# A macaron decoder trunk on one core: a fifth token-major group in place of two plain pairs, both down ranges accumulated together, and the first product between the halves of the early pair

## The chip, the cores and the metric

One Trainium2 chip, of which the program uses one core. The metric is device microseconds of one execution. A core has five engines with their own instruction queues: TensorE (PE, matrix products into PSUM banks), VectorE (DVE), ScalarE (ACT), GpSimd (POOL, here mostly an issuer of accumulating transfers) and SyncE (SP, an issuer of transfers).

## The reference

Two layers; each runs a half-step feed-forward network (FFN), a mixing of three kinds of attention, and a second FFN. The change touches the four FFNs (called a0, c0, a1 and c1 here) and one small statistic of `mem`. The sequence has 512 tokens, the model 1024 features, the hidden layer 22 tiles of 128.

```python
def _rmsnorm(t, g):
    t32 = t.astype(jnp.float32)
    t32 = t32 * lax.rsqrt(jnp.mean(t32 * t32, axis=-1, keepdims=True) + RMS_EPS)
    return t32.astype(t.dtype) * g

def _swiglu(t, w_gate, w_up, w_down):
    return (jax.nn.silu(t @ w_gate) * (t @ w_up)) @ w_down

def reference(x, mem, ...):
    mem_n = _rmsnorm(mem, mem_norm_g)
    h = x
    for l in range(DEPTH):
        f = _swiglu(_rmsnorm(h, ffn1_pre_g[l]), ffn1_w_gate[l], ffn1_w_up[l], ffn1_w_down[l])
        h = h + 0.5 * _rmsnorm(f, ffn1_post_g[l])
        ...
        f = _swiglu(_rmsnorm(h, ffn2_pre_g[l]), ffn2_w_gate[l], ffn2_w_up[l], ffn2_w_down[l])
        h = h + 0.5 * _rmsnorm(f, ffn2_post_g[l])
    return h
```

## The kernel before

**Products in three parts.** Every fp32 number is split into a high and a low part (`split`, L185: the high on ACT at L188, the low on DVE at L189), and a product is three matmuls (`mm3`, L212): high by high (L214), high by low (L215), low by high (L216). A weight tile `wh`/`wl` holds 1024 columns per partition, and the rings `wh`, `wl` and `raw` (what the transfer delivers) have four buffers each.

**Gate and up in groups.** Sixteen of the 22 hidden tiles are computed in four groups of four (`TG`, tile f to f+3; names `ta` in FFNs a, `tc` in c). A group is token-major: the tokens are the rows of the result. Gate and up together are one product of a 2 by 2 block matrix, done with seven block products in the manner of Strassen and Winograd instead of eight (`gate_up`; the products n run in `ORDER`, in the first group in `FIRST`). Each is 24 matmuls of 512 columns, 168 in a group. The block differences that products 2, 3, 5 and 6 need of the weights are made by an accumulating transfer on POOL's queue (`kt`, L318) and an addition on DVE (L344); those of the input (`ag`, from `sums`) once in each FFN on DVE and ACT. Results are gathered in tiles `c` (tag f), from PSUM banks of the ring `mm`, and multiplied by silu (L745, L756). `feature_major` then turns the group back with 16 transposes of 128 by 128 (L768), and ACT copies them to the tiles `hr` (L770).

**The rest of gate and up.** The pair of tiles 16 and 17 (`EARLY`, names `pg`, `pu`) runs first, in two halves of 256 tokens (`halved`, 96 matmuls of 256 columns each), while the second half of the tokens is still being normalised and turned (`ut`, `us`). The plain pairs 18 and 20 (`gates`, `ups`: 48 matmuls of 512 columns each) take the tokens in one go: the gates of 18 behind the early pair, its ups within the first down range, pair 20 in two parts within the second.

**Down.** Tiles 0 to 15 go back to the model's width in two ranges of eight tiles, each as seven block products of 24 matmuls (`products`, `product`; weights `wd`, block sums `bt`; factors `first_factor`, `ah`/`al`). Each range accumulates in banks of the ring `z` and adds its results to `fs` (L900 to L902). The last `down` multiplies tiles 16 to 21.

**What sets the order.** Jobs stand in a queue `Q` in the order of the last lines of `ffn` (`some`, `behind`, `add_sums`); a unit of weights is fetched and split some units ahead of its job as buffers come free. A scheduler then places the instructions on each engine, so DVE's and ACT's order follows both the queue and what it takes to be ready first. `chain` in the turns of tokens gives waits (`W_H`, `W_U`) that stand for the time from a residual to a turned tile. `mem_stats` (mean squares of `mem`, with Ln and Exp on ACT) and `mem_norm` run inside a0.

Of the kernel before, what the change touches and what calls it, by code (L numbers as in the profile page):

```python
# [22 lines left out]
def kernel(  # L23
# [79 lines left out]
    BUFS = {"u": 2, "v": 6, "q": 2, "k": 2, "o": 8, "tri": 2, "raw": 4, "rs": 1, "cs": 1, "wh": 4, "wl": 4, "f": 4}  # L103
# [410 lines left out]
    class Sub:  # L514
# [116 lines left out]


    TG = (0, 4, 8, 12)
    EARLY = NC * FC

    HR = ("o", "o", "o", "o", "o", "o", "tri", "tri")
# [3 lines left out]
    def ffn(l, src, wg, wu, wd, dst, name, spare, aside=None):  # L640
# [9 lines left out]
        def silu(f, pg):  # L650
            s = tmp(f"s{name}_{f}")
            nc.scalar.activation(s[:], pg[:], AF.Silu)
            return s

        def hidden(f, pg, pu):
            s = silu(f, pg) if pg is not None else st.pop(("silu", f))
            nc.vector.tensor_tensor(s[:], pu[:], s[:], ALU.mult)
            t = blk("q" if f < EARLY + 2 else "o", f"hid{name}_{f}")
            hid[f] = t[:, 0], t[:, 1]
            split(*hid[f], s[:])  # L660
            if f == NF - 1:
                tc.keep_in_program_order(nc.scalar.preload_act_table_set("natural_log_exp_and_others"))
# [63 lines left out]
        def gate_up(f, n, uns, last_of_top):  # L726
            seeded = ("gb", 1) in st if n == 1 else False
            if n in (0, 1, 2) and not seeded:
                st["gb", SUM[n]] = [pbank("mm", f"pt{name}_{f}_{n}_{e}") for e in range(2)]
# [10 lines left out]
            if n in (0, 2, 3, 6):  # L740
                st["c", i, j] = stile([P, 2, S], "f", f"c{name}_{f}_{i}{j}", F32)
# [12 lines left out]
            if n == 6 or n == last_of_top:  # L754
                u = st["c", i, 1]
                nc.vector.scalar_tensor_tensor(u[:], u[:], -1.0, st["c", i, 0][:], ALU.mult, ALU.mult)  # L756
                st["hid", f, i] = u

        def feature_major(f):

            for i in range(2):
                u = st.pop(("hid", f, i))
                for b in range(2):
                    f2 = f + 2 * b
                    pt = pbank("mm" if f == TG[-1] else "z", f"th{name}_{f2}_{i}")
# [6 lines left out]
                    nc.scalar.copy(pair(f2)[:, :, HALVES[i]], out_)  # L772
# [58 lines left out]
        def gates(f, ug, ahead=False):  # L831
            st[f] = [pbank("mm", f"pg{name}_{f + m}") for m in range(2)]
            for m in range(2):
                yield from gemm(st[f][m][:], ug, m, act)
                if ahead:
                    st["silu", f + m], st[f][m] = silu(f + m, st[f][m]), None

        def ups(f, uu):
            for m in range(2):
                pu = pbank("mm", f"pu{name}_{f + m}")  # L840
                yield from gemm(pu[:], uu, m, act)
                hidden(f + m, st[f][m], pu)

# [929 lines left out]
```

## Time and profile before

| | |
|---|---|
| median of 3 runs | 2379.23 us (2378.88 to 2379.49) |
| the profiled execution | 2378.61 us |
| its span | 2376.9 us, mean TensorE clock 0.998 |
| DMA | 353.92 MB, 149 GB/s on average |
| POOL busy | 189.2 us, 8% of the span |

The span is what the trace covers, and 1.7 us of the execution lie around it. In the profile's rows, "out<-in" names the tiles written and read, with a shape behind them; `x16` means so many instructions in one row. In a row of a timeline the first number is the start in us from the span's start, the second the duration; a bracket tells how long the engine had stood idle and on whom it waited. In a group's row the numbers are total busy us and mean ns of one. In a row of waits stand the total us, the number of times and the longest. A row of windows gives the window, its length, then the busy us (and counts) of PE, PEld (weight loads), DVE, ACT and POOL, the granted TensorE clock, the share of the DMA engines and GB/s. A row of issues gives the count, the size of one and the median us from issue to landing.

### The profile page before, as it was taken

What the parts mean: (1) busy time and instruction counts of PE and PEld (TensorE: products, weight loads), DVE (VectorE), ACT (ScalarE), POOL (GpSimd) and SP (SyncE); (2) the same over time, 40 slices, a digit from 0 to 9 for tenths busy, and PEclk for the clock granted to TensorE, in tenths of its full rate; (3) what the DMA queues carried; (4) which work ended last, traced back from release to release, by engine and by line L of the source; (5) the groups of instructions that cost most, each with busy time, mean ns of one, the idle gap of its engine ahead of it and who ended that gap; (6) DMA issues with size and microseconds to landing.
All of it is one profiled execution on the core that took longest, in us unless ns stands there. A gap on an engine that the chain in (4) does not pass through costs nothing.

```text
span 2376.9 us, 31030 instructions
## 1 busy us (share of the span) xinstructions
PE 2361.9 (99%) x11688; PEld 1996.9 (84%) x11688; DVE 1764.8 (74%) x2436; ACT 1410.3 (59%) x2291; POOL 189.2 (8%) x226
## 2 busy tenths in 40 slices
PE   9999999999999999999999999999999999999998
PEld 8788888888888898888888888888888888888887
DVE  8677877678776677678686788766787766767785
ACT  5656555577665555565655665656675655556654
POOL 1110000001010001100001000000001100011000
PEclk9999999999999999999999999999999999999999
DMA  6776565222223457765657656632232244586563
GB/s 213 205 203 160 152 238 151 71 72 81 76 75 115 151 160 212 190 164 160 210 153 219 178 160 192 206 111 80 63 89 81 71 133 150 161 227 163 159 168 133
DMA packets 234778, 353.92 MB, mean 149 GB/s; under 512 B 10858, under 2 KB 117634, under 8 KB 234116
## 3 DMA queue, kind: packets, MB, share of 16 engines
q1 hardware_dynamic: 208416, 301.57, 39.0%
q0 software_dynamic: 26208, 50.37, 12.4%
q8 instruction: 92, 1.51, 0.3%
q14 instruction: 58, 0.48, 0.1%
q10 hardware_dynamic: 4, 0.00, 0.0%
HBM read 337.22 MB, written 14.68 MB: 148 GB/s over the span
## 4 chain that ended last, share of the span: by engine, by line
PE 96%; DVE 1%; ACT 1%; DMA 1%; issue 0%; DVEq 0%; ACTq 0%
PE ptc L214 4%; PE ptc L216 4%; PE ptc L215 4%; PE pta L214 4%; PE pta L215 4%; PE pta L216 4%; PE pg L214 4%; PE pg L216 4%; PE pg L215 4%; PE pdc L216 3%; PE pda L216 3%; PE pdc L214 3%; PE pda L215 3%; PE pdc L215 3%; PE pda L214 3%; PE pb L214 2%
## 5 line engine op out<-in xcount | busy, mean ns | idle before, releaser
L214 PE MATMUL pg<-us_a,wh_wg 128*128 128x512 f32 x384 | 151.0, 393 | 0.0
L216 PE MATMUL pg<-us_a,wl_wg 128*128 128x512 f32 x384 | 149.7, 390 | 0.0
L215 PE MATMUL pg<-us_a,wh_wg 128*128 128x512 f32 x384 | 149.6, 390 | 0.0
L189 DVE TENSOR_TENSOR wl_tc<-ktc,wh_tc 128x1024 fp32r<-128x1024 f32 x64 | 78.3, 1223 | 54.4 <-ACT wh_tc L188 54.4
L189 DVE TENSOR_TENSOR wl_ta<-kta,wh_ta 128x1024 fp32r<-128x1024 f32 x64 | 78.3, 1223 | 51.4 <-ACT wh_ta L188 51.3
L214 PE MATMUL pta<-wh_ta,aga 128*128 128x512 f32 x256 | 101.3, 396 | 3.5 <-ACT ca L745 3.5
L214 PE MATMUL ptc<-wh_tc,agc 128*128 128x512 f32 x256 | 100.3, 392 | 0.0
L215 PE MATMUL pta<-wl_ta,aga 128*128 128x512 f32 x256 | 100.1, 391 | 0.0
L216 PE MATMUL pta<-wh_ta,aga 128*128 128x512 f32 x256 | 99.8, 391 | 0.0
L215 PE MATMUL ptc<-wl_tc,agc 128*128 128x512 f32 x256 | 99.7, 389 | 0.0
L216 PE MATMUL ptc<-wh_tc,agc 128*128 128x512 f32 x256 | 99.3, 389 | 0.0
L188 ACT CAST wh_tc<-ktc 128x1024 fp32r<-128x1024 f32 x64 | 67.5, 1055 | 53.5 <-PE ptc L216 36.5
L188 ACT CAST wh_ta<-kta 128x1024 fp32r<-128x1024 f32 x64 | 67.4, 1054 | 51.1 <-PE pta L216 35.5
L216 PE MATMUL pdc<-wh_dc,alc 128*128 128x512 f32 x224 | 87.4, 390 | 0.0
L216 PE MATMUL pda<-wh_da,ala 128*128 128x512 f32 x224 | 87.4, 390 | 0.0
L214 PE MATMUL pdc<-wh_dc,ahc 128*128 128x512 f32 x224 | 87.3, 390 | 0.0
L214 PE MATMUL pda<-wh_da,aha 128*128 128x512 f32 x224 | 87.3, 390 | 0.0
L215 PE MATMUL pdc<-wl_dc,ahc 128*128 128x512 f32 x224 | 87.2, 389 | 0.0
L215 PE MATMUL pda<-wl_da,aha 128*128 128x512 f32 x224 | 87.2, 389 | 0.0
L216 PEld LDWEIGHTS pg<-us_a,wl_wg 128*128 128x128 f32 x384 | 72.1, 188 | 15.3
L189 DVE TENSOR_TENSOR wl_tc<-raw_tc,wh_tc 128x1024 fp32r<-128x1024 f32 x48 | 58.6, 1223 | 35.2 <-ACT wh_tc L188 34.8
L215 PEld LDWEIGHTS pg<-us_a,wh_wg 128*128 128x128 f32 x384 | 72.2, 188 | 14.1
(541 smaller groups left out, 7594.4 us busy)
## 6 DMA issues: line engine op xcount, KB each, us to landing
raw_wg<-in_w_gate_dram SPq DMA_DIRECT2D x48, 512.0 KB, 3.6
raw_da<-in_ffn_w_down_dram SPq DMA_DIRECT2D x42, 512.0 KB, 3.8
raw_dc<-in_ffn_w_down_dram SPq DMA_DIRECT2D x42, 512.0 KB, 3.5
raw_ta<-in_ffn_w_gate_dram SPq DMA_DIRECT2D x36, 512.0 KB, 5.3
raw_tc<-in_ffn_w_gate_dram SPq DMA_DIRECT2D x36, 512.0 KB, 4.3
kta<-in_ffn_w_up_dram SPq DMA_DIRECT2D x32, 512.0 KB, 6.3
ktc<-in_ffn_w_up_dram SPq DMA_DIRECT2D x32, 512.0 KB, 6.4
raw_wo<-in_w_out_dram SPq DMA_DIRECT2D x24, 512.0 KB, 3.6
```

Source lines behind the costliest of these rows:

```text
L188: both = [nc.scalar.copy(h_ap, src)]
L189: make = lambda: nc.vector.tensor_tensor(l_ap, src, h_ap.bitcast(F32), ALU.subtract)
L214: nc.tensor.matmul(pt, lh, rh, start=start, stop=False, skip_group_check=free)
L215: nc.tensor.matmul(pt, lh, rl, start=False, stop=False, skip_group_check=free)
L216: nc.tensor.matmul(pt, ll, rh, start=False, stop=stop, skip_group_check=free)
```

## The change

1. `TG` has a fifth group, tiles 16 to 19. The early pair is 20 and 21. `gates`, `ups` and the plain pairs are gone. The fifth group's tiles aren't in a down range: `feature_major` splits them at once into high and low for the last `down`, in two parts, one ahead of the first down product and one behind it.
2. The products of both down ranges are interleaved (`DOWN`: n = 0 of range 0, n = 0 of range 1, n = 2 of range 0, and so on) and accumulate in the same banks, so that results leave the banks once. Both ranges' factors lie in one tile of the ring u.
3. Product 0 of the first group stands between the halves of the early pair; its banks are of the ring z, its result tile of the ring rs. Tiles 2 and 3 of the tokens get 3.0 and 4.0 more of wait where `slack` is 0.
4. The ring rs has two buffers, and holds `mem`'s rows in `mem_stats` and `mem_norm`. The table of Ln and Exp is asked for behind the last group's product 6.

```diff
-    ... "rs": 1, "cs": 1, "wh": 4, "wl": 4, "f": 4}
+    ... "rs": 2, "cs": 1, "wh": 4, "wl": 4, "f": 4}
...
-                yield ("wait", W_U[t] + self.slack)
+                yield ("wait", W_U[t] + self.slack + (W_N[t] if self.slack == 0.0 else 0.0))
...
+    W_N = (0.0, 0.0, 3.0, 4.0)
-    TG = (0, 4, 8, 12)
-    EARLY = NC * FC
-    HR = ("o", "o", "o", "o", "o", "o", "tri", "tri")
+    TG = (0, 4, 8, 12, 16)
+    EARLY = NF - 2
+    HR = 8 * ("o",)
...
-                st["gb", SUM[n]] = [pbank("mm", f"pt{name}_{f}_{n}_{e}") for e in range(2)]
+                st["gb", SUM[n]] = [pbank("z" if n == 0 and f == TG[0] else "mm", f"pt{name}_{f}_{n}_{e}") for e in range(2)]
...
-                st["c", i, j] = stile([P, 2, S], "f", f"c{name}_{f}_{i}{j}", F32)
+                st["c", i, j] = stile([P, 2, S], "rs" if n == 0 and f == TG[0] else "f", f"c{name}_{f}_{i}{j}", F32)
...
+            if n == 6 and f == TG[-1]:
+                tc.keep_in_program_order(nc.scalar.preload_act_table_set("natural_log_exp_and_others"))
-        def feature_major(f):
-            for i in range(2):
+        def feature_major(f, of=(0, 1)):
+            for i in of:
...
-                    nc.scalar.copy(pair(f2)[:, :, HALVES[i]], out_)
+                    if f2 < NC * FC:
+                        nc.scalar.copy(pair(f2)[:, :, HALVES[i]], out_)
+                        continue
+                    if i == 0:
+                        st["hl", b] = [stile([P, 2, S], "v", f"hid{name}_{f2}{x}") for x in "hl"]
+                        for m in range(2):
+                            hid[f2 + m] = tuple(t[:, m] for t in st["hl", b])
+                    split(*(t[:, :, HALVES[i]] for t in st["hl", b]), out_)
...
-        def gates(f, ug, ahead=False):
...
-        def ups(f, uu):
...
-            h, l = (stile([P, FC // 2, S // 2], "v", f"a{x}{nm}")[:] for x in "hl")
+            if ci == 0:
+                st["a", n] = stile([P, NC, 2, FC // 2, S // 2], "u", f"a{nm}")
+            h, l = (st["a", n][:, ci, x] for x in range(2))
...
-            if n in (0, 2):
-                st["b", SUM[n]] = [pbank("z", f"pd{name}_{ci}_{n}_{e}") for e in range(2)]
+            if n in (0, 2) and ci == 0:
+                st["b", SUM[n]] = [pbank("z", f"pd{name}_{n}_{e}") for e in range(2)]
...
-            opens, ends = n in (0, 2), n in (1, 4, 6)
+            opens, ends = n in (0, 2) and ci == 0, n in (1, 4, 6) and ci == NC - 1
...
+            if ci < NC - 1:
+                return
...
+        DOWN = [(n, ci) for n in ORDER for ci in range(NC)]
...
-        Q.add(ug + uu, lambda: halved(EARLY, ug, uu, 0), src.ready((0, 1)))
+        todo = turns(TG[0])
+        start = next(todo)
+        Q.add(ug + uu + start[0], lambda: halved(EARLY, ug, uu, 0), src.ready((0, 1)))
+        Q.add([], start[1])
         Q.add([], lambda: halved(EARLY, ug, uu, 1), src.ready(range(NT)))
...
-        Q.add(pairs[0][0], lambda: gates(18, pairs[0][0], True))
+        some(1)
...
-        todo = downs(0)
-        some(2)
-        behind()
+        later.clear()
+        Q.add([], lambda: feature_major(TG[-1], (0,)))
+        todo = downs()
         some(1)
-        Q.add(pairs[0][1], lambda: ups(18, pairs[0][1]))
-        some(7)
-        todo = downs(1)
-        some(3)
+        Q.add([], lambda: feature_major(TG[-1], (1,)))
+        some(12)
...
-            raw, ss = stile([P, D], "v", f"mst{t}", F32), mem_rstd[:, t]
+            raw, ss = stile([P, D], "rs", f"mst{t}", F32), mem_rstd[:, t]
```

The order of instructions at three places. First ACT in a0, between the first group's casts and the first silu of its last product (`mst` and `mem_rstd` are the statistic of `mem`, `wh_ta_4_...` the second group's weights, `ca_0_10` the first group's last result). Before:

```order
L1089 ACT_TABLE_LOAD
L1089 ACTIVATE mem_rstd<-mem_rstd 128x1
L1087 ACTIVATE mst_896,mem_rstd<-mst_896 128x1024
L188 CAST wh_ta_4_2_0_842<-kta_4_0_0_687 128x1024
L1090 ACT_TABLE_LOAD
L1090 ACTIVATE mem_rstd<-mem_rstd 128x1
L1089 ACT_TABLE_LOAD
L1089 ACTIVATE mem_rstd<-mem_rstd 128x1
L1090 ACT_TABLE_LOAD
L1090 ACTIVATE mem_rstd<-mem_rstd 128x1
L745 ACT_TABLE_LOAD
L745 ACTIVATE ca_0_10_874<-pta_0_0_0_601 128x512
```

After the change, the same stretch; the two squares of `mst` now stand some 20 rows further ahead:

```order
L188 CAST wh_ta_0_6_0_692<-kta_0_0_0_221 128x1024
L1088 ACT_TABLE_LOAD
L1088 ACTIVATE mem_rstd<-mem_rstd 128x1 x2
L1089 ACT_TABLE_LOAD
L1089 ACTIVATE mem_rstd<-mem_rstd 128x1 x2
L188 CAST wh_ta_0_6_2_699<-kta_0_0_2_230 128x1024
L188 CAST wh_ta_4_0_0_738<-raw_ta_4_0_0_613 128x1024
L188 CAST wh_ta_4_0_2_744<-raw_ta_4_0_2_619 128x1024
L129 COPY memg<-vecs_t 128x8
L130 ACTIVATE nbgate<-vecs_t 128x48
L188 CAST wh_ta_4_2_0_776<-kta_4_0_0_621 128x1024
L740 ACT_TABLE_LOAD
```

Four loads of a table and the second square between the casts became two loads, which stand together ahead of the last cast of the first group.

Second, DVE in the first group of c0, up to the input factors of products 4 and 5 (`agc_4`, `agc_5`; `rc` are sums of the input, `wl_tc_0_n` the weights of product n, `cc_0_00` the result of products 0 and 1). Before:

```order
L192 SCALAR_TENSOR_TENSOR agc_3_7946<-rc_00_7942,agc_3_7946 128x1024
L683 TENSOR_TENSOR rc_01_8015<-rc_00_7942,rc_01_8015 128x1024
L189 TENSOR_TENSOR wl_tc_0_1_0_7950<-raw_tc_0_1_0_7796,wh_tc_0_1_0_7949 128x1024
L189 TENSOR_TENSOR agc_4_8018<-rc_01_8015,agc_4_8018 128x1024
L189 TENSOR_TENSOR agc_5_8021<-rc_10_7822,agc_5_8021 128x1024
L189 TENSOR_TENSOR wl_tc_0_1_2_7956<-raw_tc_0_1_2_7802,wh_tc_0_1_2_7955 128x1024
L189 TENSOR_TENSOR wl_tc_0_2_0_8025<-ktc_0_0_0_7808,wh_tc_0_2_0_8024 128x1024
L344 TENSOR_TENSOR ktc_0_0_0_7808<-ktc_0_0_0_7808,raw_tc_0_3_0_7811 128x1024
L189 TENSOR_TENSOR wl_tc_0_2_2_8029<-ktc_0_0_2_7817,wh_tc_0_2_2_8028 128x1024
L344 TENSOR_TENSOR ktc_0_0_2_7817<-ktc_0_0_2_7817,raw_tc_0_3_2_7820 128x1024
L189 TENSOR_TENSOR wl_tc_0_3_0_8063<-ktc_0_0_0_7808,wh_tc_0_3_0_8062 128x1024
```

And now:

```order
L344 TENSOR_TENSOR ktc_0_0_2_7655<-ktc_0_0_2_7655,raw_tc_0_3_2_7658 128x1024
L192 SCALAR_TENSOR_TENSOR agc_3_7980<-rc_00_7976,agc_3_7980 128x1024
L744 TENSOR_TENSOR cc_0_00_7833<-cc_0_00_7833,ptc_0_1_0_7999 128x512
L189 TENSOR_TENSOR wl_tc_0_3_2_7993<-ktc_0_0_2_7655,wh_tc_0_3_2_7992 128x1024
L744 TENSOR_TENSOR cc_0_00_7833<-cc_0_00_7833,ptc_0_1_1_8000 128x512
L672 TENSOR_TENSOR rc_01_8028<-us_b_1_7526 128x1024
L189 TENSOR_TENSOR wl_tc_0_4_0_8038<-raw_tc_0_3_0_7649,wh_tc_0_4_0_8037 128x1024
L678 TENSOR_TENSOR rc_01_8028<-rc_00_7976,rc_01_8028 128x1024
L189 TENSOR_TENSOR wl_tc_0_4_2_8044<-raw_tc_0_3_2_7658,wh_tc_0_4_2_8043 128x1024
L189 TENSOR_TENSOR wl_tc_0_5_0_8085<-ktc_0_1_0_7988,wh_tc_0_5_0_8084 128x1024
L189 TENSOR_TENSOR agc_4_8031<-rc_01_8028,agc_4_8031 128x1024
L189 TENSOR_TENSOR agc_5_8034<-rc_10_7856,agc_5_8034 128x1024
```

The factors of products 4 and 5 stood ahead of product 2's weights; they now stand behind the weights of products 3 and 4, and the additions of product 1's result are in between.

Third, DVE at the start of the downs of c0 (`wl_dc` weights, `btc` block sums, `ac`/`alc` the lows of the factors, `asc` their sums, `hidc_16l` and `hidc_18l` the lows of the fifth group's hidden tiles). Before, around product 3 of range 0:

```order
L756 SCALAR_TENSOR_TENSOR cc_12_11_9003<-cc_12_11_9003,cc_12_10_9221 128x1024
L344 TENSOR_TENSOR btc_0_8972<-btc_0_8972,raw_dc_0_3_2_9117 128x1024
L189 TENSOR_TENSOR wl_dc_0_3_0_9233<-btc_0_8972,wh_dc_0_3_0_9232 128x1024
L192 SCALAR_TENSOR_TENSOR alc_0_3_9295<-asc_0_2_9247,ahc_0_3_9294 128x512 x2
L189 TENSOR_TENSOR wl_dc_0_3_2_9238<-btc_0_8972,wh_dc_0_3_2_9237 128x1024
L866 TENSOR_TENSOR asc_0_2_9247<-asc_0_2_9247,hrc_2_8706 128x512
L866 TENSOR_TENSOR asc_0_2_9247<-asc_0_2_9247,hrc_3_8713 128x512
L189 TENSOR_TENSOR wl_uc_18_0_9283<-raw_uc_18_0_9149,wh_uc_18_0_9282 128x1024
L189 TENSOR_TENSOR alc_0_4_9374<-asc_0_2_9247,ahc_0_4_9373 128x512 x2
```

Now, where product 2 of both ranges is prepared (the number behind `wl_dc_` is the range, the next the product):

```order
L189 TENSOR_TENSOR hidc_16l<-thc_16_1_9542,hidc_16h 128x2x256
L189 TENSOR_TENSOR hidc_18l<-thc_18_1_9549,hidc_18h 128x2x256
L189 TENSOR_TENSOR ac_0_2_9564<-asc_0_2_9565,ac_0_2_9564 128x512
L344 TENSOR_TENSOR btc_0_0_9351<-btc_0_0_9351,raw_dc_0_3_0_9391 128x1024
L189 TENSOR_TENSOR wl_dc_1_2_0_9557<-btc_1_0_9356,wh_dc_1_2_0_9556 128x1024
L344 TENSOR_TENSOR btc_0_0_9351<-btc_0_0_9351,raw_dc_0_3_2_9397 128x1024
L189 TENSOR_TENSOR wl_dc_1_2_2_9561<-btc_1_0_9356,wh_dc_1_2_2_9560 128x1024
L855 TENSOR_TENSOR asc_1_2_9608<-hrc_6_9243,hrc_4_8943 128x512
L855 TENSOR_TENSOR asc_1_2_9608<-hrc_7_9250,hrc_5_8950 128x512
L344 TENSOR_TENSOR btc_1_0_9356<-btc_1_0_9356,raw_dc_1_3_0_9430 128x1024
L189 TENSOR_TENSOR wl_dc_0_3_0_9600<-btc_0_0_9351,wh_dc_0_3_0_9599 128x1024
L189 TENSOR_TENSOR ac_0_2_9564<-asc_1_2_9608,ac_0_2_9564 128x512 x2
```

The weights of the plain pair are gone from between; the lows of the hidden tiles and a second range's weights and block sums stand ahead of the second range's factor (`ac_0_2` from `asc_1_2`).

More of the change, by code (lines that the diff above doesn't have):

```diff
@@ L932, in turns, with downs @@
             return iter(jobs)
-        def downs(ci):
-            Q.add([], lambda: iter(first_factor(ci, 0) or ()))
-            return products(ci)
+        def downs():
+            Q.add([], lambda: iter(first_factor(0, 0) or ()))
+            return products()
         ug, uu = (wpair(w[l], ND, EARLY * P, f"{x}{name}_{EARLY}") for x, w in (("g", wg), ("u", wu)))
```

71 lines of the change are left out of this document (29 added, 42 removed).

## The prediction

> **What bounds the kernel now.** I read the page's busy line and its chain first, then TensorE's waits, then the timelines where TensorE stood or where the change puts work.
>
> ```profile
> span 2376.9 us, 31030 instructions
> PE 2361.9 (99%) x11688; PEld 1996.9 (84%) x11688; DVE 1764.8 (74%) x2436; ACT 1410.3 (59%) x2291; POOL 189.2 (8%) x226
> PE 96%; DVE 1%; ACT 1%; DMA 1%; issue 0%; DVEq 0%; ACTq 0%
> ```
>
> TensorE is busy for 99% of the span and holds 96% of the chain. So a matmul removed shortens the run by its spacing, unless an engine that feeds TensorE becomes late. TensorE's own waits are few:
>
> ```profile
> PE pta L214 <- ACT ca L745: 3.5, 2, 3.0
> PE pts L1210 <- ACT ts L1241: 1.5, 2, 0.7
> PE warm L1643 <- DVE warm L1727: 1.3, 1, 1.3
> PE utx L1673 <- ACT nhx L503: 1.0, 1, 1.0
> ```
>
> One wait counts, 3.0 us in the first group of the first FFN (a0). The FFNs c0, a1 and c1 show none, and neither do the downs. What a matmul costs is its distance to the next, not the 0.39 us that its row gives:
>
> ```profile
> 1043.65 0.39 PE L214 MATMUL ptc<-wh_tc,us_b 128*128 128x512 f32 x1
> ...
> 1050.45 0.39 PE L214 MATMUL pdc<-wh_dc,ahc 128*128 128x512 f32 x1
> ```
>
> These are 30 matmuls apart: 6.80 / 30 = 0.2267 us each. A product of 24 takes 5.44 us.
>
> **What TensorE loses and gains.** The two plain pairs, 18 and 20, have 96 matmuls of 512 columns each, 192 in an FFN. They make way for a fifth group, features 16 to 19, of seven products with 24 each, 168 (the early pair moves from 16 to 20 and keeps its size). So 24 fewer in each of four FFNs, 96 in all: 96 x 0.2267 = **-21.8 us**. A token-major group must be turned back:
>
> ```profile
> 103.36 1.91 PE L768 MATMUL tha<-ident,ca 128*128 128x128 f32 x16
> 105.03 0.48 PE L214 MATMUL pta<-wh_ta,aga 128*128 128x512 f32 x1
> ```
>
> 16 transposes take 105.03 - 103.36 = 1.67 us; four FFNs: **+6.7 us**. The downs keep their 14 products and the last down its 144 matmuls; that both ranges meet in one bank pair removes copies and adds from ACT and DVE, and nothing from TensorE. The mixing part has the same order on TensorE.
>
> **The wait in a0.**
>
> ```profile
> 92.12 0.39 PE L216 MATMUL pta<-wh_ta,us_x 128*128 128x512 f32 x1
> 95.55 0.50 PE L214 MATMUL pta<-wh_ta,aga 128*128 128x512 f32 x1 [3.04 <-ACT ca L745]
> ...
> 98.00 0.63 PE L216 MATMUL pta<-wh_ta,aga 128*128 128x512 f32 x1
> 98.43 0.63 PE L214 MATMUL pta<-wh_ta,aga 128*128 128x512 f32 x1
> ...
> 100.39 0.39 PE L216 MATMUL pta<-wh_ta,aga 128*128 128x512 f32 x1
> ```
>
> ```profile
> 75.28 3.93 SPq L1086 DMA_DIRECT2D mst<-in_mem_dram  x2
> ...
> 83.28 1.06 ACT L1087 ACTIVATE mst<-mst 128x1024 f32<-128x1024 f32 x1 [3.84 <-DMA mst<-in_mem_dram]
> ...
> 85.56 1.28 ACT L1089 ACT_TABLE_LOAD   x1
> ...
> 88.00 1.04 ACT L188 CAST wh_ta<-kta 128x1024 fp32r<-128x1024 f32 x1
> ...
> 93.61 1.28 ACT L745 ACT_TABLE_LOAD   x1
> 94.90 0.60 ACT L745 ACTIVATE ca<-pta 128x512 f32<-128x512 f32 x1
> ```
>
> From 92.12 to 100.39 stand 12 matmul starts, which need 12 x 0.2267 = 2.72 us and take 8.27: 5.55 lost, 3.5 of it waiting and the rest at a slower spacing (98.00 to 98.43). The cause is on ACT: the squares of mem come late behind their transfers (issued at 75.28, the first used at 83.28), and five table loads of 1.28 us stand from 85.56 to 94.90 ahead of the silu that frees the banks. In the changed order the squares stand early, among the work of the early pair, two table loads serve the whole statistic, and the next group's opening product no longer needs the banks that this silu frees, since the first group's sum 0 lies in the other ring. I take all of it: **-5.5 us** (bounds 0 to -5.5).
>
> The Trainium skill ("TensorE: Matmul & The Clock Gate", Part 1) says that an idle window of about 3.4 us halves TensorE's clock until about as long a busy one has passed. The row agrees: after 3.04 us the spacing is 0.43, nearly double, for some 3 us. By that rule, waits of 1 us, as I expect below, cost no clock; the sum has no term for it.
>
> **What the feeders have to do.** DVE writes every low half. Its mean durations and its spacing differ:
>
> ```profile
> L189 DVE TENSOR_TENSOR wl_dc<-raw_dc,wh_dc 128x1024 fp32r<-128x1024 f32 x42 | 51.3, 1223 | 25.2 <-ACT wh_dc L188 25.0
> L189 DVE TENSOR_TENSOR alc<-hrc,ahc 128x512 fp32r<-128x512 f32 x24 | 16.0, 686 | 1.7 <-ACT ahc L188 1.3
> ```
>
> ```profile
> 871.16 1.22 DVE L677 TENSOR_TENSOR rc<-us_b 128x1024 f32<-128x1024 f32 x1
> 872.29 2.35 DVE L189 TENSOR_TENSOR wl_gc<-raw_gc,wh_gc 128x1024 fp32r<-128x1024 f32 x2
> 874.56 2.35 DVE L189 TENSOR_TENSOR wl_tc<-raw_tc,wh_tc 128x1024 fp32r<-128x1024 f32 x2
> 876.83 2.35 DVE L677 TENSOR_TENSOR rc<-us_b 128x1024 f32<-128x1024 f32 x2
> ...
> 1090.09 1.28 DVE L902 TENSOR_TENSOR fc<-fc,pdc 128x512 f32<-128x512 f32 x2
> 1091.29 0.68 DVE L189 TENSOR_TENSOR alc<-hrc,ahc 128x512 fp32r<-128x512 f32 x1
> ```
>
> Back to back, four of 1024 columns take 4.54 us, 1.135 each, and two of 512 take 1.20, 0.60 each.
>
> *Downs.* Each range has 14 weight lows, 4 block sums (L344), 14 factor lows and 8 factor sums. Both ranges, 4 adds of results, 4 new lows of hidden features and the group's last multiply: 37 x 1.135 + 52 x 0.60 = 73.2 us, against 14 x 5.44 = 76.2 us of TensorE. Before, plain pairs stood between the products:
>
> ```profile
> 1079.00:1118.00 39.00, 39.00 (x173) 32.07 (x172) 33.86 (x42) 23.64 (x32) 4.79 (x4) 1.00 0.73 189
> 1118.00:1129.00 11.00, 11.00 (x50) 9.11 (x49) 10.40 (x14) 5.31 (x8) 0.00 (x0) 1.00 0.33 97
> 1129.00:1150.00 21.00, 21.00 (x94) 17.39 (x93) 13.37 (x14) 11.54 (x15) 0.00 (x0) 1.00 0.44 146
> ```
>
> (PE is the second number, DVE the fourth.) DVE had 33.86 of 39 us of products and room behind them (13.37 of 21). Now it is at 96% for 76 us. The head is the tight place. Behind the group's last product, ACT has two silu, a table load of 1.28 and the highs of the hidden features and of the next factor. DVE, from its last multiply to the first low that range 1's second factor needs, has 9 instructions of 1024 and 11 of 512 in the changed order: 9 x 1.135 + 11 x 0.60 = 16.8 us. It starts about 1.4 late (two silu of 0.6) and waits about another 1 for ACT's highs behind the table load, so that low is ready some 19.3 us after the group. TensorE has eight transposes twice (0.84 each) and three products in that time, 18.0, and wants the low at its third matmul, 18.5. I take 0.9 there and 0.4 in the next product, whose lows follow in the same queue: 1.3 for each FFN, **+5.2 us** (bounds 0, if ACT's part overlaps, to 4.7 each, the first rival's price). Queued behind a late low on DVE are the following product's, and TensorE alone waits for them.
>
> *First group of c0, a1, c1.* In c0 before:
>
> ```profile
> 868.80 0.93 PE L614 MATMUL utb<-ident,fb 128*128 128x128 f32 x7
> ...
> 870.04 2.12 PE L825 MATMUL pgc<-us_b,w_gc 128*128 128x256 f32 x16
> ...
> 881.60 0.40 PE L214 MATMUL pgc<-us_b,wh_gc 128*128 128x512 f32 x1
> ```
>
> ```profile
> 877.00:905.00 28.00, 28.00 (x143) 23.77 (x142) 25.09 (x25) 13.93 (x17) 4.81 (x4) 1.00 0.77 212
> ```
>
> The second half of the early pair began at 870.04 and took 11.56 us. Now product 0 stands ahead of it: it begins at 875.4 and ends at 887.0, products 1, 2 and 3 end at 903.3, and product 4 wants the low of its factor 0.8 later, at 904.1. DVE had 25.09 of 28 us to do there, with a plain pair as cover; now the cover is product 0, 5.4 us. In the changed order 22 instructions of 1024 and 6 of 512 stand on DVE from the first sum of the turned input to that low. That sum begins at about 876.6: the last token tile is now turned behind 18 of product 0's matmuls, at about 874, and the first sum followed its turn by some 2.4 us before (868.80 to 871.16). So 22 x 1.135 + 6 x 0.60 = 28.6, ready at 905.2. **+1.1 us** each, +3.3 in all (bounds 0, if one sum is made earlier, to 3.5 each, below).
>
> *Start of a0.* The first group's blocks are now cast before the early pair's second half, one cast of 1.04 us (ACT's row at 88.00) ahead of the square of the last token tile: **+0.7 us** (0 to 2).
>
> *Transfers.* Product 0's two fetches move on SP's queue from behind pair 18's gates to ahead of the early pair's first half, and POOL's first additions with them; the fifth group adds four accumulating transfers on POOL in each FFN, 16 in all.
>
> ```profile
> raw_tc<-in_ffn_w_gate_dram SPq DMA_DIRECT2D x36, 512.0 KB, 4.3
> kta<-in_ffn_w_up_dram POOLq DMA_DIRECT2D x16, 512.0 KB, 9.0
> ```
>
> They land in 4.3 to 9.0 us and are asked for two products (10.9 us) ahead, in stretches where the DMA engines' share is 0.77 (877 to 905). So they cost nothing, with TensorE's work on the products in hand as cover; one that came two products late would cost its landing, up to 9 us.
>
> Sum: -21.8 + 6.7 - 5.5 + 5.2 + 3.3 + 0.7 = -11.4. The profiled execution took 2378.61 (1.7 outside the span), the median is 0.6 above: 2378.6 - 11.4 + 0.6 = 2367.8, so **2368 us**.
>
> **Rivals.** *Lows without overlap (slower).* If DVE in the dense stretches goes by durations (1.223 and 0.686), because each low waits for its high on ACT and so starts afresh, the downs need 37 x 1.223 + 52 x 0.686 = 80.9, 4.7 over TensorE's 76.2, 18.8 in all; the first groups need 31.0, 3.5 late, 10.5 in all. -21.8 + 6.7 - 5.5 + 18.8 + 10.5 + 0.7 = +9.4: 2389. It decides from a spacing of about 1.18 on, where the sum is zero. For it: wl_dc waited 25.0 us for ACT in 42 lows. Against it: DVE was busy 10.40 of 11 us from 1118 without TensorE waiting.
> The Trainium skill ("VectorE: DVE Perf Modes", The DRAIN you can't avoid) has the next instruction start only when the pipe is empty, unless it is not held; taken strictly that is this rival. The rows at 872.29 to 876.83 speak against the strict form.
>
> *Downs' head worse.* Each FFN loses 3.8 instead of 1.3 there, since factors and hidden lows share DVE: +10, 2378. For it: 96% load with four weight buffers. Against: the later products have slack.
>
> *a0's wait stays or moves.* The scaling of mem's second tile, now in a0's first group on DVE, waits for a transfer into the one of two buffers that the squares free late; what is queued behind it is the second low of product 2. A late landing there, or a silu still late, costs what the wait cost: +5.5, 2373. Against: fewer table loads, and by the rows the squares of before waited 3.84 us for such a transfer that was asked for only 8 us ahead.
>
> *No new wait at all:* -21.8 + 6.7 - 5.5 = -20.6, 2358.6. For it: TensorE before waited nowhere outside a0 and the mixing.
>
> **How the numbers follow.** Forecast 0.50 (alone 2363 to 2372), no new wait 0.15, a0's wait 0.12, downs' head 0.13, lows without overlap 0.10. A measurement of this kernel tells 0.2%, 4.8 us, from no change: faster is below 2374.5. Forecast and no new wait lie there, most of a0's case and a part of the head's: 0.78. Same 0.13, mostly the head's. Slower 0.09. The range 2358 to 2380 takes in all but the slower rival.
>
> **What would show it.** TensorE busy down by about 15 us and 96 fewer L214 to L216 of 512 columns; no wait for a silu in a0; in the first groups a wait of about 1 us for agc's low at product 4, in the downs one for the factor low of range 1's second product. Wrong would be: TensorE waits above 3 us in an FFN for DVE's wl of the downs, a DVE busy share near 100% there, or a wait for a transfer.

## The result, and the profile after

| | before | after |
|---|---|---|
| median of 4 runs, us | 2379.06 (2377.94 to 2379.49) | 2363.7 (2363.13 to 2364.29) |
| profiled execution, us | 2378.61 | 2364.29 |

The ratio is 0.9936, with a 95% interval of 0.9919 to 0.9953: 15.4 us faster, where 2368.0, a gain of 11.4 in the sum, was forecast. The page of the changed kernel (span and instructions, busy time of each engine, shares of the chain that ended last):

```profile
span 2362.2 us, 31098 instructions
PE 2348.4 (99%) x11656; PEld 1984.4 (84%) x11656; DVE 1778.4 (75%) x2436; ACT 1440.2 (61%) x2329; POOL 213.0 (9%) x242
PE 91%; DVE 4%; DMA 2%; ACT 1%; issue 1%; POOL 0%; SPq 0%; DVEq 0%; POOLq 0%; ACTq 0%
```

TensorE has 32 instructions fewer (96 matmuls out, 64 transposes in), and is busy for 13.5 us less (2.0 of it the slower spacing in a0 before). The chain now leaves TensorE for 9% of the span instead of 4%, so the feeders have come closer. TensorE's waits after (total us, times, longest):

```profile
PE pts L1209 <- ACT ts L1240: 1.5, 2, 0.7
PE warm L1642 <- DVE warm L1726: 1.3, 1, 1.3
PE pga L829 <- ACT us_x L191: 1.1, 1, 1.1
PE pta L216 <- DVE aga L189: 0.9, 1, 0.9
PE pdc L216 <- DVE ac L189: 0.7, 2, 0.3
PE pda L216 <- DVE aa L189: 0.7, 2, 0.3
```

The 3.0 us for the silu `ca` is gone. In its place stand small waits for lows of factors: `aga` in a0's first group, and `ac` or `aa` in the downs of all four FFNs, at the place that was forecast. TensorE's timeline at the head of c0's downs (start, duration):

```profile
1074.06 1.03 PE L765 MATMUL thc<-ident,cc 128*128 128x128 f32 x8
...
1092.16 0.39 PE L214 MATMUL pdc<-wh_dc,ac 128*128 128x512 f32 x1
1092.38 0.39 PE L215 MATMUL pdc<-wl_dc,ac 128*128 128x512 f32 x1
1092.61 0.39 PE L214 MATMUL pdc<-wh_dc,ac 128*128 128x512 f32 x1
1092.84 0.39 PE L215 MATMUL pdc<-wl_dc,ac 128*128 128x512 f32 x1
1093.57 0.72 PE L216 MATMUL pdc<-wh_dc,ac 128*128 128x512 f32 x2 [0.34 <-DVE ac L189]
```

From 1092.84 to 1093.57 are 0.73 us for one spacing of 0.227: 0.50 lost (the bracket shows only the part in which the array stood empty). It happens once in each FFN, in range 1's product 2, whose first matmul is that at 1092.16. What DVE did until then, from the group's last multiply on:

```profile
1076.47 1.22 DVE L751 SCALAR_TENSOR_TENSOR cc<-cc,cc 128x1024 f32<-128x1024 f32 x1
1077.74 0.69 DVE L189 TENSOR_TENSOR hidc_16l<-thc,hidc_16h 128x512 fp32r<-128x512 f32 x1
...
1091.70 1.22 DVE L189 TENSOR_TENSOR wl_dc<-btc,wh_dc 128x1024 fp32r<-128x1024 f32 x1
1092.83 1.28 DVE L189 TENSOR_TENSOR ac<-asc,ac 128x512 fp32r<-128x512 f32 x2
```

And one view of windows for the whole of c0's downs (length, then busy us and counts of PE, PEld, DVE, ACT, POOL), and one at the times of c0's first group that the prediction quoted from before (c0 now starts 5.45 earlier, so the same times show work that much further on):

```profile
1071.50:1147.00 75.50, 75.16 (x339) 61.74 (x339) 70.96 (x85) 51.06 (x68) 5.98 (x5) 1.00 0.73 204
```

```profile
877.00:905.00 28.00, 28.00 (x142) 23.68 (x142) 28.00 (x29) 16.53 (x20) 1.23 (x2) 1.00 0.36 119
```

DVE is at 71.0 of 75.5 us in the downs (94%, forecast 96%), and in the first group at 28.00 of 28, where it was at 25.09 (the window 5.45 earlier, 871.55 to 899.55, shows 28.00 too). TensorE loses nearly nothing in either, so a saturated feeder is not yet a wait. ACT in a0, where the statistic of `mem` and its tables now stand:

```profile
39.45 1.06 ACT L1086 ACTIVATE mst<-mst 128x1024 f32<-128x1024 f32 x1
...
46.85 1.06 ACT L1086 ACTIVATE mst<-mst 128x1024 f32<-128x1024 f32 x1 [3.86 <-DMA mst<-in_mem_dram]
...
65.46 1.28 ACT L1088 ACT_TABLE_LOAD   x1
66.76 0.30 ACT L1088 ACTIVATE mem_rstd<-mem_rstd 128x1 f32<-128x1 f32 x2
67.07 1.28 ACT L1089 ACT_TABLE_LOAD   x1
...
77.61 1.28 ACT L740 ACT_TABLE_LOAD   x1
78.90 0.60 ACT L740 ACTIVATE ca<-pta 128x512 f32<-128x512 f32 x1
```

The second square still waits 3.9 us for its transfer, but 30 us ahead of the silu; two loads serve the statistic.

Where the time came from, by FFN (first to last matmul of each, us). The changed kernel's second profiled execution is that of a later experiment:

| | a0 | c0 | a1 | c1 |
|---|---|---|---|---|
| before | 349.17 | 338.61 | 336.85 | 337.18 |
| after | 342.84 | 335.71 | 333.86 | 334.33 |
| after, second profile | 341.83 | 336.20 | 333.95 | 334.23 |

Each of c0, a1 and c1 gives 2.4 to 3.0, a0 gives 6.3 and 7.3. The mixing parts are as long as before within 0.5.

### The profile page after: what moved, and what is told of

Same layout as the page of the kernel before. It is cut to its first block, busy times and chain, and to the rows that moved or that the text cites. A ratio compares the mean times of both kernels' runs of the same rounds, so it can differ in the third digit from the quotient of the medians.

```text
span 2362.2 us, 31098 instructions
## 1 busy us (share of the span) xinstructions
PE 2348.4 (99%) x11656; PEld 1984.4 (84%) x11656; DVE 1778.4 (75%) x2436; ACT 1440.2 (61%) x2329; POOL 213.0 (9%) x242
## 4 chain that ended last, share of the span: by engine, by line
PE 91%; DVE 4%; DMA 2%; ACT 1%; issue 1%; POOL 0%; SPq 0%; DVEq 0%; POOLq 0%; ACTq 0%
PE ptc L216 5%; PE ptc L215 5%; PE ptc L214 5%; PE pta L216 5%; PE pta L214 5%; PE pta L215 5%; PE pg L216 3%; PE pg L214 3%; PE pg L215 3%; PE pdc L216 3%; PE pda L216 3%; PE pdc L214 3%; PE pdc L215 3%; PE pda L215 3%; PE pda L214 3%; PE pb L214 2%
## 5 line engine op out<-in xcount | busy, mean ns | idle before, releaser
L214 PE MATMUL pg<-us_a,wh_wg 128*128 128x512 f32 x384 | 150.9, 393 | 0.0
L216 PE MATMUL pg<-us_a,wl_wg 128*128 128x512 f32 x384 | 149.7, 390 | 0.0
L215 PE MATMUL pg<-us_a,wh_wg 128*128 128x512 f32 x384 | 149.6, 390 | 0.0
L216 PE MATMUL pta<-wh_ta,aga 128*128 128x512 f32 x320 | 124.6, 390 | 0.9 <-DVE aga L189 0.9
L214 PE MATMUL ptc<-wh_tc,agc 128*128 128x512 f32 x320 | 125.2, 391 | 0.0
L214 PE MATMUL pta<-wh_ta,aga 128*128 128x512 f32 x320 | 125.2, 391 | 0.0
L215 PE MATMUL ptc<-wl_tc,agc 128*128 128x512 f32 x320 | 124.5, 389 | 0.0
L215 PE MATMUL pta<-wl_ta,aga 128*128 128x512 f32 x320 | 124.5, 389 | 0.0
L216 PE MATMUL ptc<-wh_tc,agc 128*128 128x512 f32 x320 | 124.5, 390 | 0.0
L189 DVE TENSOR_TENSOR wl_ta<-raw_ta,wh_ta 128x1024 fp32r<-128x1024 f32 x60 | 73.1, 1222 | 38.1 <-ACT wh_ta L188 38.1
L215 PE MATMUL ptc<-wl_tc,us_b 128*128 128x512 f32 x240 | 93.6, 390 | 0.0
L214 PE MATMUL ptc<-wh_tc,us_b 128*128 128x512 f32 x240 | 93.5, 391 | 0.0
L216 PE MATMUL ptc<-wh_tc,us_b 128*128 128x512 f32 x240 | 93.1, 389 | 0.0
L188 ACT CAST wh_tc<-raw_tc 128x1024 fp32r<-128x1024 f32 x60 | 62.9, 1052 | 46.8 <-PE ptc L216 40.1
L188 ACT CAST wh_ta<-raw_ta 128x1024 fp32r<-128x1024 f32 x60 | 62.9, 1052 | 43.6 <-PE pta L216 38.3
L216 PE MATMUL pdc<-wh_dc,ac 128*128 128x512 f32 x224 | 87.4, 392 | 0.7 <-DVE ac L189 0.7
L216 PE MATMUL pda<-wh_da,aa 128*128 128x512 f32 x224 | 87.4, 392 | 0.7 <-DVE aa L189 0.7
```

Of the source, the lines that this page charges most:

```text
L188: both = [nc.scalar.copy(h_ap, src)]
L189: make = lambda: nc.vector.tensor_tensor(l_ap, src, h_ap.bitcast(F32), ALU.subtract)
L214: nc.tensor.matmul(pt, lh, rh, start=start, stop=False, skip_group_check=free)
L215: nc.tensor.matmul(pt, lh, rl, start=False, stop=False, skip_group_check=free)
L216: nc.tensor.matmul(pt, ll, rh, start=False, stop=stop, skip_group_check=free)
```

## The experiments

Experiments of one group ran on one chip, beside runs of the kernel before; every ratio is to that kernel there (medians 2379.48, 2379.8 and 2379.78 in the three groups). "Over the changed kernel" means over its first median, 2363.7, taken beside a before of 2379.06; the befores differ by up to 0.7 us, so differences of that size tell nothing. None leaves out part of the computation.

**What ended a0's wait.** *mst_v*: the changed kernel with the rows of `mem` for the statistic (`mem_stats`) in the ring v again.

```diff
-            raw, ss = stile([P, D], "rs", f"mst{t}", F32), mem_rstd[:, t]
+            raw, ss = stile([P, D], "v", f"mst{t}", F32), mem_rstd[:, t]
```

> The changed kernel, but mem's two rows lie in the ring v again, so that their squares, Ln and Exp stand on ACT where they stood before the change. If the early squares and the two table loads took the wait in a0 away: it comes back, 3 to 5.5 us, 2367 to 2369 us. If the banks did it (the next group's opening product no longer needs the banks that the late silu frees): no wait for that silu, 2362.5 to 2364.

Measured: 2367.02 (2365.66 to 2370.32), ratio 0.9948 (0.9933 to 0.9963), 3.3 us over the changed kernel. The squares are late again, and with them the tables. ACT's timeline of this kernel:

```profile
77.76 1.06 ACT L1086 ACTIVATE mst<-mst 128x1024 f32<-128x1024 f32 x1 [6.03 <-DMA mst<-in_mem_dram]
...
81.01 1.28 ACT L1088 ACT_TABLE_LOAD   x1
...
82.42 1.03 ACT L188 CAST wh_ta<-kta 128x1024 fp32r<-128x1024 f32 x1
83.46 1.28 ACT L740 ACT_TABLE_LOAD   x1
```

TensorE's rows there, of those that waited:

```profile
83.50 0.51 PE L214 MATMUL pta<-wh_ta,aga 128*128 128x512 f32 x1 [1.57 <-ACT wh_ta L188]
84.75 0.50 PE L215 MATMUL pta<-wl_ta,aga 128*128 128x512 f32 x1 [0.75 <-DVE wl_ta L189]
```

TensorE now waits for the cast of weights that stands on ACT behind the square and the table, no longer for the silu that frees banks; some 9 us later, behind three more table loads, it loses another 0.7 for a copy of `ca` and 0.5 for a `wl_ta`. That the squares stand early is thus shown to be what removes the wait. That the loss is smaller than before's 5.5 may be due to product 0's sum in the ring z, but no run changes that alone.

*before_rs*: the kernel before with this one part of the change, two buffers in the ring rs and the rows of `mem_stats` there.

> The kernel before, with only the ring rs at two buffers and mem's rows of the statistic in it. If the place of the squares is the cause of the wait in a0: it goes, -5 us, 2373 to 2375 us. If the banks are: the wait stays, 2378 to 2380.

Measured: 2373.69 (2372.92 to 2373.99), ratio 0.9976 (0.9966 to 0.9986): 5.8 us faster, where the prediction's term was 5.5. The wait for `ca` is absent from its list. ACT's squares stand at 21.46 and 23.86 there, and no table load for Ln or Exp stands behind them. This small edit is over a third of the whole gain.

**The interleaved ranges.** *ranges_apart*: the changed kernel with one range after the other, each with its own banks, copies and adds.

```diff
-        DOWN = [(n, ci) for n in ORDER for ci in range(NC)]
+        DOWN = [(n, ci) for ci in range(NC) for n in ORDER]
...
-            opens, ends = n in (0, 2) and ci == 0, n in (1, 4, 6) and ci == NC - 1
+            opens, ends = n in (0, 2), n in (1, 4, 6)
...
-            if ci < NC - 1:
-                return
```

> The changed kernel, but the two down ranges one behind the other, each with its own banks and its own copies and adds of results (12 more adds of 512 columns on DVE in an FFN). If DVE's load in the downs is what counts: 71.0 + 12 x 0.60 = 78.2 us against 75.5 of TensorE, 2.5 to 4 us more in each FFN, 2374 to 2380 us. If DVE has room enough: 2363 to 2366, and the interleaving isn't what the change needs.

Measured: 2392.64 (2390.74 to 2395.08), ratio 1.0054 (1.0039 to 1.0069): slower than before, 29 us over the changed kernel, far beyond what either theory gave. The FFNs are 347.21, 343.18, 341.47 and 341.56. TensorE's timeline of this kernel at the head of c0's downs:

```profile
1084.84 1.03 PE L765 MATMUL thc<-ident,cc 128*128 128x128 f32 x8
1089.34 0.79 PE L214 MATMUL pdc<-wh_dc,ac 128*128 128x512 f32 x1 [3.46 <-DVE hidc_16l L189]
1089.93 0.63 PE L215 MATMUL pdc<-wl_dc,ac 128*128 128x512 f32 x1
1090.35 0.63 PE L216 MATMUL pdc<-wh_dc,ac 128*128 128x512 f32 x1
```

Product 2 of range 0 opens new banks of the ring z right behind the second turn of the fifth group, and those banks hold the turned tiles until DVE has written `hidc_16l` and `hidc_18l` from them. In the changed kernel range 1's product 0 stands at that place; it goes on in banks that it has, and covers DVE's work. Behind the wait TensorE's spacing is 0.43 for some 3 us (granted clock 0.50 from 1089.2 to 1092.6). A second wait follows in range 1 (1.7 us for `ac` at 1147.66): the factor's sums on DVE stand among adds of results that the shared banks save, and its high on ACT behind a cast of weights. The edit also gives each product's factors a whole tile of the ring u, but no wait of the factors for such a tile shows in the trace. So the shared banks do save time, though the prediction gave them nothing on TensorE.

**The first product's place.** *p0_behind*: product 0 behind both halves of the early pair, and the added waits `W_N` at zero. The last input sums then stand ahead of product 1, as in *sums_ahead* below.

```diff
-        Q.add(ug + uu + start[0], lambda: halved(EARLY, ug, uu, 0), src.ready((0, 1)))
-        Q.add([], start[1])
+        Q.add(ug + uu, lambda: halved(EARLY, ug, uu, 0), src.ready((0, 1)))
         Q.add([], lambda: halved(EARLY, ug, uu, 1), src.ready(range(NT)))
-        some(1)
+        Q.add(*start)
...
+        some(1)
```

> The changed kernel, but product 0 of the first group behind both halves of the early pair, with the added waits of tiles 2 and 3 at zero. If its place between the halves only delays the input's first sum on DVE: the waits at product 4 go (0.16 in each of three FFNs, 1.06 in a0), 2361.5 to 2363.5 us. If it covers the turn of the last token tiles: waits for us or ut ahead of the second half, 1 to 3 us in each of c0, a1, c1, 2367 to 2373.

Measured: 2376.78 (2373.53 to 2379.03), ratio 0.9986 (0.9977 to 0.9996): 13 us over the changed kernel. The profiled execution was the fastest of the ten, 2373.53, and its trace shows 9.1 of the 13 in the span; what the others lost beyond it isn't shown. In it both theories looked at the wrong place: c0, a1 and c1 are as fast (335.56, 333.97, 334.08, and their waits at product 4 are gone, as with sums_ahead's order), and all of the loss is in a0, 352.19, which is 9.4 over 342.84. There transfers come late. SP's issues of a weight tile for the first group's product 3, and behind it of the second tile for product 2, of this kernel:

```profile
35.98 0.37 SPq L318 DMA_DIRECT2D raw_ta<-in_ffn_w_up_dram  x1
36.40 0.46 SPq L318 DMA_DIRECT2D kta<-in_ffn_w_up_dram  x1
```

and of the changed kernel:

```profile
22.19 0.37 SPq L318 DMA_DIRECT2D raw_ta<-in_ffn_w_up_dram  x1
22.66 0.42 SPq L318 DMA_DIRECT2D kta<-in_ffn_w_up_dram  x1
```

14 us later. SP waits for a raw buffer, and the four are full of the weights of products 0 and 1 until DVE writes their lows. The changed kernel writes product 0's at 20.91 and 22.11, p0_behind all four from 34.73 on:

```profile
34.73 4.62 DVE L189 TENSOR_TENSOR wl_ta<-raw_ta,wh_ta 128x1024 fp32r<-128x1024 f32 x4
```

POOL's accumulating transfer, the cast and the low follow late, and TensorE waits (of p0_behind):

```profile
PE pta L215 <- DVE wl_ta L189: 5.1, 3, 2.6
...
PE pta L214 <- ACT wh_ta L188: 1.4, 2, 1.2
```

These are 6.5 us. The granted clock was also 0.52 from 54.2 to 57.6 and from 61.0 to 64.4, with a spacing of 0.43, which costs some 1.6 us each time. Against that stands the changed kernel's own 1.06 us for `aga`, which p0_behind doesn't have. The sums' order isn't the cause of the loss: in sums_ahead a0 gains.

*wn0* takes the four waits `W_N` alone to zero:

> The changed kernel without the added 3.0 and 4.0 of wait for token tiles 2 and 3. If product 0 between the halves is only placed well with them: TensorE turns tile 2 or 3 before it is normalised, waits for fb, 1 to 4 us in c0, a1 and c1 each, 2367 to 2374. If they change nothing that TensorE sees: 2363 to 2365.

Measured: 2363.88 (2361.78 to 2364.73), ratio 0.9932 (0.9919 to 0.9946), no difference from the changed kernel.

**Room on DVE in the downs.** *lows_7* writes the low of one half of range 1's factors a second time, seven more operations of 512 columns in an FFN, 4.2 us of DVE by the prediction's 0.60; *lows_14* does so in both ranges. They change no value.

```diff
                 split(h[:, two], l[:, two], from_, scale=-1.0 if n == 3 else None)
+                if b == 0 and ci == 1:
+                    hf32 = h[:, two].bitcast(F32)
+                    if n == 3:
+                        nc.vector.scalar_tensor_tensor(l[:, two], from_, -1.0, hf32, ALU.mult, ALU.subtract)
+                    else:
+                        nc.vector.tensor_tensor(l[:, two], from_, hf32, ALU.subtract)
```

> The changed kernel with 7 lows of range 1's factors written twice in each FFN, 512 columns each. DVE was busy 71.0 of the 75.5 us of the downs; 7 x 0.60 = 4.2 more makes 75.2. If the downs are within a few us of DVE's bound, as the sum says: 0.5 to 2 us more in each FFN, 2365.5 to 2371 us. If DVE has far more room: 2363.5 to 2364.5. If DVE goes by its durations and is at its bound already: 4.8 more in each FFN, 2383.

> The same with 14 lows written twice in each FFN, of both ranges: 71.0 + 14 x 0.60 = 79.4 us of DVE against 75.5. If the downs are within a few us of DVE's bound: 3.5 to 5 us more in each FFN, 2377 to 2384 us. If DVE has far more room: below 2368. If DVE is at its bound already: 9 in each FFN, 2400.

Measured: lows_7 2377.21 (2373.1 to 2380.67), ratio 0.999 (0.9981 to 0.9999); lows_14 2389.52 (2386.44 to 2392.2), ratio 1.0041 (1.0026 to 1.0056). Both cost more than the first theory said and less than the last. In lows_7 the forecast's wait of 0.50 grows at the same matmul. TensorE in c0, and then in a1:

```profile
1098.42 0.74 PE L216 MATMUL pdc<-wh_dc,ac 128*128 128x512 f32 x2 [2.69 <-DVE ac L869]
...
1099.94 0.63 PE L214 MATMUL pdc<-wh_dc,ac 128*128 128x512 f32 x1
1100.37 0.63 PE L215 MATMUL pdc<-wl_dc,ac 128*128 128x512 f32 x1
```

```profile
1438.09 0.74 PE L216 MATMUL pda<-wh_da,aa 128*128 128x512 f32 x2 [2.69 <-DVE aa L869]
1438.66 0.39 PE L214 MATMUL pda<-wh_da,aa 128*128 128x512 f32 x1
1438.89 0.40 PE L215 MATMUL pda<-wl_da,aa 128*128 128x512 f32 x1
```

The second write of the wanted low stands on DVE behind the other half's low and a low of weights, so one of the seven costs 2.35 us (0.60 + 1.135 + 0.60), the wait growing to 2.85: by its place, more than by its own 0.60. The products behind it absorb the other six. Then comes the clock: in c0 the spacing is 0.43 for about 3.5 us after the wait (granted clock 0.50 from 1099.4 to 1102.8), in a1 after the same wait it is not (1.00 from 1438.1 to 1441.5). Against the changed kernel c0 lost 3.75 us (339.46), a1 2.17 (336.03) and c1 4.98 (339.31): 1.6 to 2.8 us hang on the clock in an FFN. That this is also the spread between this kernel's executions is likely by its size, but one profile doesn't show it. In lows_14 each FFN waits two or three times (the longest 2.2 to 2.4). So the head of the downs has nothing to spare, and behind it there is room for the other six operations of lows_7, but not for all of lows_14's.

**Can the last waits go?** *sums_ahead* puts all sums of the input ahead of the group (`some(9)` behind the second `add_sums`, none between):

> The changed kernel, but the input's last sums and factors (products 4 and 5) stand ahead of product 1 in the queue. If the waits at product 4 (0.16 in c0, a1, c1 and 1.06 in a0) are DVE's order: they go, -1 to -1.5 us, 2362 to 2363 us. If DVE's amount of work in the first group is what counts: the wait moves to product 2's or 3's weights, 2363.5 to 2366.

Measured: 2367.81 (2365.88 to 2369.07), ratio 0.9952 (0.9936 to 0.9969). a0 gains (341.67, its wait for `aga` is gone), but c0, a1 and c1 lose 0.6 to 0.7 each: product 3's weights come late there instead, the second theory. (These are figures of the fastest execution, 2365.88; what the others lost more isn't shown.) *best_a* does it in a0 alone:

> The changed kernel with the last input sums ahead of product 1 in a0 alone. If a0's 1.06 at product 4 is the order on DVE behind its own waits there, and c0, a1, c1 keep the order that gave 0.16: -1.0 to -1.2 us against the changed kernel on the same chip, 2362 to 2363. If it comes back elsewhere, as the reordering in the other FFNs did: no difference.

Measured: 2363.54 (2362.35 to 2364.0), ratio 0.9931 (0.9919 to 0.9944), no difference. *fact_early* makes both ranges' factors for a product together, which is one product earlier for range 1:

```diff
-            at = DOWN.index((n, ci)) + 1
-            if at < len(DOWN):
-                first_factor(*reversed(DOWN[at]))
+            if n == 0 and ci == 0:
+                first_factor(1, 0)
+            if n < 6 and ci == NC - 1:
+                for c2 in range(NC):
+                    first_factor(c2, ORDER[ORDER.index(n) + 1])
```

> The changed kernel, but the factors of both ranges for the next n are made together, a product earlier for range 1, so that on DVE the second factor's lows stand ahead of block sums and weights of product 3. If the wait of 0.50 us in each FFN is the order on DVE: it goes, -2 us, 2361.5 to 2362.5 us. If DVE's amount of work at the head is what counts: the wait moves to the weights of the next product, 2363 to 2365.

Measured: 2373.53 (2371.42 to 2374.51), ratio 0.9973 (0.9962 to 0.9984), 10 us over the changed kernel. The 0.50 at product 2 is gone and comes back larger at product 3, with a spacing of 0.43 behind it in c0 and a1. So the wait moved, as the second theory has it, but to the next factor instead of its weights, and at far above that theory's price. TensorE in c0 of this kernel:

```profile
1099.00 0.50 PE L214 MATMUL pdc<-wh_dc,ac 128*128 128x512 f32 x1 [1.71 <-ACT ac L191]
...
1101.17 1.22 PE L216 MATMUL pdc<-wh_dc,ac 128*128 128x512 f32 x2 [0.97 <-DVE ac L192]
```

*best_b* is best_a with range 1's factor sums for product 2 (L855) on POOL instead of DVE:

> The same, and two of the four factor sums at the head of the downs (range 1, product 2) made on POOL in place of DVE, 1.2 us less for DVE in front of the late low. If DVE's amount of work at the head is what counts: the waits of 0.50 in each FFN go, 1.5 to 2 us less than without, 2360.5 to 2361.5. If POOL's sums come late behind its queue of accumulating transfers, or hold DVE up: waits for as of POOL, 2363 or more.

Measured: 2365.5 (2364.52 to 2367.11), ratio 0.994 (0.9928 to 0.9953), about 2 us over the changed kernel. The wait at product 2 is gone and about 1 us or more stands at product 3. POOL's row of this kernel, and then DVE's at the same time:

```profile
1075.05 4.00 POOL L855 TENSOR_TENSOR asc<-hrc,hrc 128x512 f32<-128x512 f32 x2
```

```profile
1075.57 2.31 DVE L751 SCALAR_TENSOR_TENSOR cc<-cc,cc 128x1024 f32<-128x1024 f32 x1
```

DVE's multiply takes 2.31 us beside POOL's sums instead of 1.22 (the row at 1076.47 of the changed kernel), so 1.1 of the 1.2 us that left DVE were paid back at once.

*after_again* is the changed kernel once more, in the group of the last three:

> The changed kernel itself once more, on the same chip as the next three: 2363 to 2365 us. If its first four runs were a lucky state of the clock or of transfers: above 2366.

Measured: 2363.09 (2362.91 to 2364.8), ratio 0.9932 (0.9919 to 0.9944). In its profile the 1.06 us for `aga` in a0 are absent, one of the downs' heads loses 0.97 instead of 0.50, and the span is 2361.0. So best_a had no such wait to remove. The wait can be followed back in the traces: in the first profile ACT's second square of `mst` got its transfer at 46.85, the high of an `aga` stands right behind it (47.91), and DVE, idle until that high, then works without a gap from 48.98 to the late low at 60.48. In the second profile that transfer was issued 2.3 us earlier (38.33 against 40.62), and the square, at 45.08, and the low, at 58.70, came 1.8 earlier; in wn0's the square stands at 46.33 and the wait's bracket is 0.5 instead of 0.9. So the square that was moved forward costs a0 up to 1.06 us by its transfer. Waits of this size come and go between executions, by about 1 us each. No version was found that beats the changed kernel.

## Why the prediction was right, point by point

The forecast's mechanism held: fewer matmuls, a0's wait gone, and new waits at the two places named. The time lay 4.3 below it, since the new waits were priced too high, at 8.5 us where 2.5 came. The step on shared banks was wrong and the one on transfers incomplete (below); that neither shows in the time is luck, as the change has what both need.

- **Matmuls and transposes (-15.1).** Counted as forecast: 96 matmuls of 512 columns fewer and 64 transposes more. TensorE's busy time fell by 13.5 in this profile and by 14.8 in the second (2347.1); it holds the 2.0 of a0's slower spacing too, so the count bears this term out better than the busy time.
- **a0's wait (-5.5).** Shown by before_rs, -5.8. Of its reasons, the early squares decide (mst_v, before_rs); what the banks add wasn't tested alone.
- **The downs' head (+5.2).** The right matmul and the right low; the size was 0.50 in each FFN, 2.0 in all. DVE was timed well: from its last multiply to the start of that low 16.36 us, and the low's own 0.6 make 17.0, against 16.8. The multiply began 2.4 after the group instead of 1.4, and the wait of 1 for ACT's highs did not come, so that the low was ready 19.4 after the group's end (at 1074.06), forecast 19.3: two errors of 1 us that cancelled, which is luck. What failed is the other side: TensorE's order has a second L214 and L215 ahead of the first L216 (the rows from 1092.16), so it wanted the low at the product's fifth matmul and not its third, 19.0 after the group instead of 18.5. The 0.4 in the next product was not there. fact_early, lows_7 and lows_14 show that the low of this factor and the load behind it are what bounds. The margin is small: the same wait lost 0.97 in one FFN of the second profile, and 2.85 in lows_7.
- **First groups of c0, a1, c1 (+3.3).** 0.16 each, 0.5 in all, at product 4 as forecast (899.05 - 898.66 is 0.39, a spacing of 0.227 and 0.16). From the first sum to the low of that factor DVE took 28.6 us, as forecast. TensorE's two rows in c0, then DVE's:

```profile
898.66 0.39 PE L215 MATMUL ptc<-wl_tc,agc 128*128 128x512 f32 x1
899.05 0.73 PE L216 MATMUL ptc<-wh_tc,agc 128*128 128x512 f32 x2
```

```profile
870.34 2.35 DVE L672 TENSOR_TENSOR rc<-us_b 128x1024 f32<-128x1024 f32 x2
...
896.65 1.21 DVE L189 TENSOR_TENSOR wl_tc<-ktc,wh_tc 128x1024 fp32r<-128x1024 f32 x1
897.78 2.34 DVE L189 TENSOR_TENSOR agc<-rc,agc 128x1024 fp32r<-128x1024 f32 x2
```

  (897.78 - 870.34 + 1.135.) But it began 0.8 sooner than the step had it: c0 starts 5.45 earlier than before (851.35 against 856.80), which puts the forecast's 876.6 at 871.15. And again TensorE has a second L214 and L215 ahead of the first L216, and asks for the low at its fifth matmul. The bound of 0 was the right side. The step left out a0's own first group, where the same factor was 1.06 late in one profile of two.
- **Start of a0 (+0.7).** 0.5, as a wait of the last turn for `fx`.
- **Transfers (0).** Right, but for a reason that the step did not name. The cover was there because product 0's early place empties raw buffers; without it transfers come 14 us late and a0 loses 9.4 in the profiled execution (p0_behind).
- **Shared banks (nothing on TensorE).** Wrong for the parts together: with the fifth group's turned tiles in the same ring, the old order of the ranges would have cost 29 us (ranges_apart). The sum was not hurt, since the change does both at once.

The account by the measured sizes: -15.1 - 5.5 + 2.0 + 0.5 + 0.5, and 0.3 for a turn of `mem` behind the downs of a0, that was in no step, make -17.3. The profiled spans fell by 14.7 and 15.9. Of the difference in the first, 1.1 are the wait for `aga`, and 0.7 a slower start of the program, ahead of any of the changed work, that the second profile lacks; the mixing's 0.4 goes the other way. Some 0.2 in each of c0, a1 and c1 and 0.4 in a0 I could not assign to a row; that is left open.

Of the rivals, *no new wait* (2358.6) was nearly as close as the forecast, 5.1 away against 4.3. *Lows without overlap* fell: over 28 us in which DVE was never idle its operations of 1024 columns start 1.135 apart with durations of 1.21. The Trainium skill ("VectorE: DVE Perf Modes", The DRAIN you can't avoid) was read strictly for that rival; the exception that it makes for an operation that is not held agrees with these rows. *a0's wait stays or moves* came at most with the 1.06 for `aga`, and by the second square's transfer, not by the scaling that it names. *Downs' head worse* did not come. lows_7 came near its time (2377) with 4.2 us of DVE more in an FFN, but by the place of one operation and by the clock.

## What to carry to other kernels

A feeder at 94 to 100% of a stretch is no loss by itself: find the one operand that is wanted next, count the feeder's instructions to it from the last thing that held it up, and read from the order at which matmul of the product it is first used. Before taking work off such an engine or reordering it, see whose buffers and banks the present place of a job frees: here the first group's product 0 and range 1's product 0, both seemingly mere shifts, carried the transfers of a0 and the banks of the downs. A statistic whose transfer comes late can hold up another engine's queue for microseconds, and moving it to a buffer that is free early was worth a third of this change by itself.

## What the runs showed of the hardware

- Waits of TensorE of 2.69 us were followed by a spacing of 0.43 instead of 0.227 in c0 of lows_7 (granted clock 0.50), and not in a1 after the same wait (1.00); a wait of 2.63 us in a0 of p0_behind, at 96.00, wasn't either. Waits up to 1.06 us cost no clock in the changed kernel. The Trainium skill ("TensorE: Matmul & The Clock Gate", Part 1) gives an idle window of about 3.4 us for it; here shorter ones did it, and the measurement decides. The slower spacing added 1.6 to 2.8 us to a wait where it came.
- An operation of POOL on 128x512 fp32 took 2.0 us, and DVE's operation beside it 2.31 instead of 1.22. The Trainium skill ("SBUF — State Buffer", Who interferes with whom) has the two share a port pair, which agrees.
